# Strassen sums of the activations made beside the second branch and kept in memory

## The chip, the cores and the metric

The kernel runs on one core of a Trainium2 chip. The metric is the device time of one execution in microseconds, the median of several runs. A profiled execution gives a trace, from which a page and the answers to questions are made; its times are microseconds unless marked ns.

Engines are named as in the profile: PE multiplies matrices, DVE (VectorE) and ACT (ScalarE) work on elements, SP only issues transfers here, and ACT issues some as well. SPq and ACTq are those issuing queues.

## The reference

The reference is one layer of an encoder over two sequences, a prompt of 512 and a sample of 256 tokens, each with 16 learned tokens in front, at width 2048:

```python
def mixer_layer(z, norm_g, w_in, ...):
    h = rmsnorm(z, norm_g)
    cols = h @ w_in
    u_a, gate_a, q_b, k_b, v_b, gate_b, glr_b, x_c, gate_c, merge = split_cols(cols)
    y_a = s5_mixer(u_a, ...) * jax.nn.silu(gate_a)
    y_b = gla_mixer(q_b, k_b, v_b, glr_b, ...) * jax.nn.silu(gate_b)
    y_c = rglru_mixer(x_c, ...) * jax.nn.silu(gate_c)
    gates = jax.nn.sigmoid(merge).reshape(bsz, length, N_BRANCH, D_MODEL)
    m = (gates[:, :, 0] * (y_a @ w_out_a) + gates[:, :, 1] * (y_b @ w_out_b)
         + gates[:, :, 2] * (y_c @ w_out_c))
    return z + m @ w_o
```

A final rmsnorm follows, and the learned tokens are dropped. `merge` alone has 3 x 2048 columns, which are 48 of the 84 column blocks of 128 of the input projection.

## The kernel before

Everything is kept transposed: 128 channels on the partitions, tokens along a row. The normalised activations are 16 chunks of 128 channels, each as two tiles `xh[k]` and `xl[k]` of a rounded type (the value is hi + lo), with 784 columns: 16 learned tokens and 768 others. A product with weights takes three matmuls: hi by hi, lo by hi, hi by lo. `split` makes the two parts: ACT copies the value into hi, DVE subtracts hi from the value into lo. The activations are also kept in memory unsplit, as `xnorm` (16 x 128 x 768).

The program runs in stages: input projection and normalisation; branch one (`branch_s5`); branch two (`branch_gla`); branch three (`branch_lru`); the Strassen pairs (`strassen`); the merge of the branches and the output projection (`merge_and_project`).

The 36 column blocks of the branches and the 48 merge blocks are computed in two ways.

- A merge tile (`fill_step`, line 273) is one column block by all 16 chunks: 16 steps of 6 matmuls of 384 columns into two PSUM banks, 96 in all. Its result goes to `gspill` in memory. Such tiles are used to fill PE's time: `tick` puts a step in during branch one at a rate set by `FILLS` (the rates of branches two and three are 0), and `cover` puts in a number of steps outright, such as `LT` = 39 near the end of branch three.
- A Strassen pair is two column blocks at once. Chunks k and k + 8 and the two halves of the 768 columns make a 2 x 2 matrix of blocks, and seven products in place of eight give both results: 4 steps (`sb`) of 7 x 2 x 3 = 42 matmuls, 168 in all, into seven PSUM banks (`products`, line 1149). The eight pairs of gate blocks come first, then `NST` pairs of merge blocks: 8 + 15 = 23. The other 18 merge blocks are merge tiles.

The pairs need four sums of activation blocks for each k from 0 to 7: `sh[0]`, `sh[1]`, `sh[2]` (and `sl`) and a last one, which takes the place of the second half of `xh[k]` and `xl[k]` once the merge tiles no longer need it. `strassen` makes them on DVE, with splits, from `xnorm` loads issued at line 1581, while `cover` lets PE run the remaining merge tiles. Then each step's weights are loaded at line 1615 (`raw`, two buffers), three of them split into hi and lo, and four sums of weights (`t`) split as well; hi and lo have three buffers. Steps are prepared two or three ahead.

A scheduler orders each engine's instructions from the order of the code, and each engine and each issuing queue then runs its own list strictly in order. Transfers of SP carry eight completion counters in turn, so at most eight are under way. A tile whose memory was another tile's waits for the last use of that one.

After the last pair, 16 loads of 192 KB (line 1674) bring back eight branch results into the memory of the sums, they are split, and the merge begins at line 1292.

The functions that the change touches, and what calls them:

Of the kernel before, what the change touches and what calls it, by code (L numbers as in the profile page):

```python
# [6 lines left out]
F32 = mybir.dt.float32  # L7
F32R = mybir.dt.float32r
I32 = mybir.dt.int32
AF = mybir.ActivationFunctionType  # L10
ALU = mybir.AluOpType
# [5 lines left out]
NT = NP_ + NS  # L17
# [3 lines left out]
HN = NT // 2  # L21
# [5 lines left out]
NST = 15  # L27
# [4 lines left out]
XS = 2  # L32
# [63 lines left out]
def build(tc, A, out_p, out_s):  # L96
# [9 lines left out]
    yspill = drm.tile([16, 128, NT], F32, name="yspill")  # L106
    hspill = drm.tile([16, 128, NT], F32, name="hspill")
    zspill = drm.tile([8, 128, NS], F32, name="zspill")
    xnorm = drm.tile([16, 128, NT], F32, name="xnorm")

# [628 lines left out]
def branch_gla(E):  # L739
    tc, A = E["tc"], E["A"]  # L740
    V, S, PE, SP = E["V"], E["S"], E["PE"], E["SP"]
    col, split, proj, evac, tick, psB = (E[k] for k in ("col", "split", "proj", "evac", "tick", "psB"))
# [11 lines left out]
    def tmp():  # L754
        return lp.tile([128, T], F32, name="tmp", bufs=4)

# [25 lines left out]
    for hp in range(2):  # L782
# [139 lines left out]
        for h in range(2):  # L922
# [22 lines left out]
            tick()  # L945
    lp.release()
# [613 lines left out]
def strassen(E):  # L1560
# [11 lines left out]
    sh, sl = [[None] * 8 for i in range(3)], [[None] * 8 for i in range(3)]  # L1572
    for k in range(8):
        for i in range(3):
            sh[i][k] = sp.tile([128, HN], F32R, name=f"sh{i}{k}")
            sl[i][k] = sp.tile([128, HN], F32R, name=f"sl{i}{k}")
    xp = tc.alloc_tile_pool(name="stx", bufs=1, reuse_waits="tile")

    def load(k, o, n, **kw):
        x = xp.tile([128, n], F32, **kw)  # L1580
        (S if k % 8 < XS else SP).dma_start(x[:], xnorm[k, :, o:o + n])
        return x[:]

    def sums(k):
        xa = load(k, 0, NT, name="xa", bufs=2)
        s_, x, u = load(k + 8, HN, HN, name="x", bufs=2), xa[:, :HN], xa[:, HN:]
        V.tensor_tensor(out=s_, in0=s_, in1=u, op=add)
        split(sh[0][k][:], sl[0][k][:], s_)
        V.tensor_tensor(out=s_, in0=s_, in1=x, op=sub)
        split(sh[1][k][:], sl[1][k][:], s_)  # L1590
        V.tensor_tensor(out=u, in0=u, in1=x, op=sub)
        split(sh[2][k][:], sl[2][k][:], u)

    def last_sum(k):

        x = load(k + 8, 0, HN, name="x", bufs=2)
        s_ = xp.tile([128, HN], F32, name="y", bufs=2)[:]
        V.tensor_tensor(out=s_, in0=sh[1][k][:].bitcast(F32), in1=sl[1][k][:].bitcast(F32), op=add)
        V.tensor_tensor(out=s_, in0=x, in1=s_, op=sub)
        split(xh[k][:, t2], xl[k][:, t2], s_)  # L1600

    n = max(1, len(merges))
    for k in range(8):
        sums(k)
        while len(merges) > max(1, n * (7 - k) // 8):
            E["cover"](16)
    E["cover"](16 * len(merges) + 16)

    xp.release()
    tp = tc.alloc_tile_pool(name="stt", bufs=1, reuse_waits="tile")  # L1610
    xp = tc.alloc_tile_pool(name="sty", bufs=2, reuse_waits="tile")
# [14 lines left out]
    def operand(a, k):  # L1626
        if isinstance(a, int):
            return sh[a][k][:], sl[a][k][:]
        tk, ts = k + 8 * (a[1] == "2"), t1 if a[0] == "1" else t2
        return xh[tk][:, ts], xl[tk][:, ts]  # L1630

    ahead = []
    for sb in range(4):
        if sb < 3:
            ahead.append(weights(0, sb))
        last_sum(2 * sb)
        last_sum(2 * sb + 1)
    xp.release()
# [28 lines left out]
    free = [f"s{p}{i}{k}" for k in range(8) for i in range(3) for p in "hl"]  # L1667
    yh, yl = [], []
    for k in range(8):
        h = E["act"].tile([128, NT], F32R, name=f"h{8 + k}")  # L1670
        l = E["act"].tile([128, NT], F32R, name=f"l{8 + k}")
        for o in (0, HN):
            yr = sp.tile([128, HN], F32, name=free.pop(0))
            SP.dma_start(yr[:], E["yspill"][k, :, o:o + HN])
            split(h[:, o:o + HN], l[:, o:o + HN], yr[:])
        yh.append(h)
        yl.append(l)
# [118 lines left out]
```

## Time and profile before

| | us |
|---|---|
| median of three runs | 2037.04 |
| lowest and highest run | 2035.94, 2038.36 |
| the profiled execution: time | 2038.42 |
| the profiled execution: span of the trace | 2036.6 |
| PE busy in the span | 2003.8 (98%) |
| DVE busy | 1504.9 (74%) |
| ACT busy | 808.2 (40%) |

The span lies inside the time: 1.8 us of the profiled execution are outside it. Busy time of PE counts overlapping matmuls once. The stages in this trace: branch one to about 404 us, branch two to about 610, branch three to about 800, the pairs from 842 to 1518, then the rest.

### The profile page before, as it was taken

The numbers are of one execution on the slowest core, as the hardware profiler recorded it, in microseconds if no ns is written. First come the engines' busy times: TensorE is split into PE (matmuls) and PEld (weight loads), VectorE is DVE, ScalarE is ACT, GpSimd is POOL, SyncE is SP. The second block draws the span as 40 slices with busy tenths as digits, with TensorE's granted clock in tenths as the row PEclk, the third lists the DMA queues.
The fourth block names the chain that finished last, engine by engine and source line by source line (L and its number), as shares of the span: only waits on it lengthen the run. The fifth ranks groups of instructions, "written<-read, shape, count | busy, mean of one in ns | idle before, by whom it ended". The sixth has DMA issues, their size and how long they took to land.

```text
span 2036.6 us, 30982 instructions
## 1 busy us (share of the span) xinstructions
PE 2003.8 (98%) x12228; PEld 1972.5 (97%) x12228; DVE 1504.9 (74%) x2784; ACT 808.2 (40%) x1172; POOL 0.2 (0%) x4
## 2 busy tenths in 40 slices
PE   8999999999999999999999999999999999999997
PEld 8999999999989999999999999999999999999997
DVE  8988983656567876977676656665669989887778
ACT  7332111443437675433333222222235435533345
POOL 0000000000000000000000000000000000000000
PEclk9999999999999999999999999999999999999999
DMA  8762234421111323543443222322355335532256
GB/s 292 251 123 94 75 102 120 147 80 49 61 52 45 102 72 122 179 133 102 139 135 112 94 94 100 103 91 100 104 183 215 125 114 180 176 117 94 94 163 218
DMA packets 105378, 252.12 MB, mean 124 GB/s; under 512 B 18960, under 2 KB 39952, under 8 KB 105232
## 3 DMA queue, kind: packets, MB, share of 16 engines
q1 hardware_dynamic: 77072, 200.61, 30.8%
q10 hardware_dynamic: 28160, 49.53, 6.9%
q8 instruction: 96, 1.57, 0.3%
q14 instruction: 50, 0.41, 0.1%
HBM read 200.65 MB, written 49.45 MB: 123 GB/s over the span
## 4 chain that ended last, share of the span: by engine, by line
PE 78%; DVE 13%; ACT 4%; DMA 3%; issue 1%; ACTq 0%; SPq 0%; DVEq 0%
PE pm L1149 24%; PE br L1149 23%; PE pm L199 10%; PE pm L273 5%; PE br L1422 4%; PE pm L1292 2%; PE br L1292 2%; DVE sc L61 2%; DVE W L61 2%; PE pm L332 2%; DVE lo L61 2%; ACT gt L89 1%; DMA c<-gspill 1%; DVE hb L61 1%; PE br L199 1%
## 5 line engine op out<-in xcount | busy, mean ns | idle before, releaser
L89 ACT ACTIVATE hi<-raw 128x768 fp32r<-128x768 f32 (+2 forms) x234 | 216.1, 924 | 482.8 <-PE br L1149 129.0
L61 DVE TENSOR_TENSOR lo<-raw,hi 128x768 fp32r<-128x768 f32 (+2 forms) x234 | 246.3, 1053 | 131.5 <-ACT hi L89 131.1
L61 DVE TENSOR_TENSOR lo<-t,hi 128x1024 fp32r<-128x1024 f32 x140 | 171.5, 1225 | 193.4 <-ACT hi L89 193.2
L89 ACT ACTIVATE hi<-t 128x1024 fp32r<-128x1024 f32 x140 | 148.4, 1060 | 279.6 <-PE pm L1149 138.3
L1149 PE MATMUL pm<-l,hi 128*128 128x384 f32 (+1 forms) x616 | 197.3, 320 | 0.0
L1149 PE MATMUL pm<-h,hi 128*128 128x384 f32 (+1 forms) x616 | 196.6, 319 | 0.2 <-ACT g L89 0.2
L1149 PE MATMUL pm<-h,lo 128*128 128x384 f32 (+1 forms) x616 | 196.6, 319 | 0.0
L1149 PE MATMUL br<-l,hi 128*128 128x384 f32 (+1 forms) x504 | 167.1, 331 | 0.0
L1149 PE MATMUL br<-h,hi 128*128 128x384 f32 (+1 forms) x504 | 165.9, 329 | 0.0
L1149 PE MATMUL br<-h,lo 128*128 128x384 f32 (+1 forms) x504 | 165.8, 329 | 0.0
L199 PE MATMUL pm<-h,hi 128*128 128x392 f32 (+1 forms) x608 | 161.8, 344 | 1.2 <-ACT xp L1022 1.2
L199 PE MATMUL pm<-h,lo 128*128 128x392 f32 (+1 forms) x608 | 159.5, 342 | 1.0 <-DVE lo L61 1.0
L199 PE MATMUL pm<-l,hi 128*128 128x392 f32 (+1 forms) x608 | 159.6, 341 | 0.0
L273 PE MATMUL pm<-h,lo 128*128 128x384 f32 x512 | 131.6, 338 | 2.5 <-DVE lo L61 2.5
L273 PE MATMUL pm<-h,hi 128*128 128x384 f32 x512 | 133.8, 342 | 0.0
L273 PE MATMUL pm<-l,hi 128*128 128x384 f32 x512 | 132.6, 340 | 0.0
L1149 PEld LDWEIGHTS pm<-h,hi 128*128 128x128 f32 x616 | 115.7, 188 | 0.7 <-ACT g L89 0.5
L1149 PEld LDWEIGHTS pm<-h,lo 128*128 128x128 f32 x616 | 116.0, 188 | 0.0
L1149 PEld LDWEIGHTS pm<-l,hi 128*128 128x128 f32 x616 | 115.7, 188 | 0.0
L199 PEld LDWEIGHTS pm<-h,hi 128*128 128x128 f32 x608 | 111.0, 188 | 2.7 <-ACT xp L1022 1.5
L199 PEld LDWEIGHTS pm<-h,lo 128*128 128x128 f32 x608 | 111.2, 188 | 1.5 <-DVE lo L61 1.3
L199 PEld LDWEIGHTS pm<-l,hi 128*128 128x128 f32 x608 | 110.6, 188 | 0.2
(358 smaller groups left out, 4799.6 us busy)
## 6 DMA issues: line engine op xcount, KB each, us to landing
raw<-in_w_st SPq DMA_DIRECT2D x92, 512.0 KB
raw<-in_w_in SPq DMA_DIRECT2D x74, 512.0 KB
gspill<-g ACTq DMA_DIRECT2D x48, 384.0 KB
raw<-in_w_ost SPq DMA_DIRECT2D x32, 512.0 KB
xr<-in_xT SPq DMA_DIRECT2D x31, 392.0 KB
m<-gspill SPq DMA_DIRECT2D x26, 384.0 KB
raw<-in_w_out SPq DMA_DIRECT2D x16, 512.0 KB
raw<-in_w_outc SPq DMA_DIRECT2D x16, 512.0 KB
```

Of the source, the lines that this page charges most:

```text
L61: return f(*a, **k)
L89: ins = self.eng.activation(**k)
L199: PE.matmul(ps[h][:, :nw], w[:, k, :], xx[kt][:, n0 + h * nw:n0 + (h + 1) * nw], start=(kt == 0 and j == 0), stop=(kt == 15 and j == 2))
L273: PE.matmul(ps[h][:, :HN], w[:, k % 8, :], xx[k][:, NM + h * HN:NM + (h + 1) * HN], start=(k == 0 and j == 0), stop=(k == 15 and j == 2))
L332: PE.matmul(ps0[2 * t + h][:, :HT], w[:, k, :], xx[kt][:, h * HT:(h + 1) * HT], start=(kt == 0 and j == 0), stop=(kt == 15 and j == 2))
L1149: PE.matmul(ps[j][:, :nt], w[:, wi, kk, :], x, start=(k == 0 and q == 0), stop=(k == n - 1 and q == 2))
L1292: PE.matmul(ps[h][:, :HN], w[:, 4 * b + k, :], yy[4 * b + k][:, h * HN:(h + 1) * HN], start=(k == 0 and j == 0), stop=(k == 3 and j == 2))
L1422: PE.matmul(po[:, :NS], x[:, n, :], y[k][:, ss], start=(first and j == 0), stop=(last and j == 2))
```

## The change

The four sums of each k are made in branch two, by the new `strassen_sums`, which is called at every third `tick` of that branch: it loads two chunks of `xnorm`, makes the sums in place in two tiles of 768 columns (`pa`, `pb`), splits each (hi into `ph`, lo in place) and stores the four parts in memory (`sspill`). At the pairs, `fetch` loads three split sums of each k into new tiles (`s1h`, `s1l`, and `s2h`, `s2l` with two sums side by side), and `fetch_last` loads the fourth into the second half of `xh[k]` and `xl[k]`. The sums on DVE between branch three and the pairs are gone, with their covers. `NST` is 16: 16 merge tiles in place of 18, and 24 pairs in place of 23. After the pairs, eight loads of 384 KB bring back the branch results into the `s2` tiles.

```diff
-NST = 15
+NST = 16
-XS = 2
...
+    sspill = drm.tile([8, 2, 2, 128, NT], F32, name="sspill")
...
+    def strassen_sums(k):
+        a, b = (lp.tile([128, NT], F32, name=n) for n in ("pa", "pb"))
+        SP.dma_start(a[:], E["xnorm"][k])
+        SP.dma_start(b[:], E["xnorm"][k + 8])
+        t1, t2 = slice(0, HN), slice(HN, NT)
+        TT = lambda o, x, y, op: V.tensor_tensor(out=o, in0=x, in1=y, op=op)
+        TT(b[:, t2], b[:, t2], a[:, t2], ALU.add)
+        TT(a[:, t2], a[:, t2], a[:, t1], ALU.subtract)
+        TT(a[:, t1], b[:, t2], a[:, t1], ALU.subtract)
+        TT(b[:, t1], b[:, t1], a[:, t1], ALU.subtract)
+        for i, x in enumerate((a, b)):
+            h = lp.tile([128, NT], F32R, name="ph")
+            S.activation(out=h[:], in_=x[:], func=AF.Copy)
+            TT(x[:].bitcast(F32R), x[:], h[:].bitcast(F32), ALU.subtract)
+            SP.dma_start(E["sspill"][k, i, 0], h[:].bitcast(F32))
+            SP.dma_start(E["sspill"][k, i, 1], x[:])
+
+    beside = [k for k in range(8)]
+    ticks = [0]
+
+    def tick():
+        E["tick"]()
+        ticks[0] += 1
+        if ticks[0] % 3 == 0 and beside:
+            strassen_sums(beside.pop(0))
...
-    def sums(k):
-        xa = load(k, 0, NT, name="xa", bufs=2)
-        s_, x, u = load(k + 8, HN, HN, name="x", bufs=2), xa[:, :HN], xa[:, HN:]
-        V.tensor_tensor(out=s_, in0=s_, in1=u, op=add)
-        split(sh[0][k][:], sl[0][k][:], s_)
-        V.tensor_tensor(out=s_, in0=s_, in1=x, op=sub)
-        split(sh[1][k][:], sl[1][k][:], s_)
-        V.tensor_tensor(out=u, in0=u, in1=x, op=sub)
-        split(sh[2][k][:], sl[2][k][:], u)
...
+    def fetch(k):
+        s1[k] = [sp.tile([128, HN], F32R, name=f"s1{p}{k}") for p in "hl"]
+        s23[k] = [sp.tile([128, 2, HN], F32R, name=f"s2{p}{k}") for p in "hl"]
+        for p in range(2):
+            SP.dma_start(s1[k][p][:].bitcast(F32), spill[k, 1, p, :, HN:])
+            SP.dma_start(s23[k][p][:].bitcast(F32), spill[k, 0, p].rearrange("q (i n) -> q i n", i=2))
+
+    def fetch_last(k):
+        for p, x in enumerate((xh, xl)):
+            SP.dma_start(x[k][:, t2].bitcast(F32), spill[k, 1, p, :, :HN])
+
     for k in range(8):
-        sums(k)
-        while len(merges) > max(1, n * (7 - k) // 8):
-            E["cover"](16)
+        fetch(k)
     E["cover"](16 * len(merges) + 16)
...
-        last_sum(2 * sb)
-        last_sum(2 * sb + 1)
+        fetch_last(2 * sb)
+        fetch_last(2 * sb + 1)
...
-        for o in (0, HN):
-            yr = sp.tile([128, HN], F32, name=free.pop(0))
-            SP.dma_start(yr[:], E["yspill"][k, :, o:o + HN])
-            split(h[:, o:o + HN], l[:, o:o + HN], yr[:])
+        yr = sp.tile([128, NT], F32, name=f"s2{'hl'[k % 2]}{k // 2}")
+        SP.dma_start(yr[:], E["yspill"][k])
+        split(h[:], l[:], yr[:])
```

SP's list at the hand-over from branch three to the pairs, before: `in_w_in` are merge tile weights, `xnorm` the activations for the sums, `in_w_st` the weights of a pair's step, in the order of the steps.

```order
L135 DMA raw<-in_w_in 128x1024 x8
L1581 DMA xa<-xnorm 128x768
L1581 DMA x<-xnorm 128x384
L1581 DMA xa<-xnorm 128x768
L1581 DMA x<-xnorm 128x384
L1615 DMA raw<-in_w_st 128x1024
L1581 DMA xa<-xnorm 128x768
L1581 DMA x<-xnorm 128x384
L1581 DMA xa<-xnorm 128x768
L1581 DMA x<-xnorm 128x384
L1615 DMA raw<-in_w_st 128x1024
```

The same place of the changed kernel, its beginning: the weights of the first two steps, the last sums of chunks 0 to 4 (`l_104` and `h_103` are `xl[0]` and `xh[0]`, and so on), and the first of the other sums.

```order
L135 DMA raw<-in_w_in 128x1024 x4
L1623 DMA raw<-in_w_st 128x1024 x2
L1614 DMA l_104<-sspill 128x384
L1614 DMA h_103<-sspill 128x384
...
L1614 DMA h_206<-sspill 128x384
L1614 DMA l_207<-sspill 128x384
L1608 DMA s1h_7668<-sspill 128x384
L1609 DMA s2h_7670<-sspill 128x768
L1608 DMA s1l_7669<-sspill 128x384
L1609 DMA s2l_7671<-sspill 128x768
```

And its end, where the loads of the sums of chunk 7, the 29th to 32nd, are followed by the weights of the third step, the last sums of chunks 5 to 7, and the weights of the fourth and later steps.

```order
L1608 DMA s1h_7724<-sspill 128x384
L1609 DMA s2h_7726<-sspill 128x768
L1608 DMA s1l_7725<-sspill 128x384
L1609 DMA s2l_7727<-sspill 128x768
L1623 DMA raw<-in_w_st 128x1024
L1614 DMA h_227<-sspill 128x384
L1614 DMA l_228<-sspill 128x384
L1614 DMA h_248<-sspill 128x384
L1614 DMA l_249<-sspill 128x384
L1614 DMA h_269<-sspill 128x384
L1614 DMA l_270<-sspill 128x384
L1623 DMA raw<-in_w_st 128x1024 x5
```

Weights of steps stood between the loads before; now those of the third step stand behind all 32 loads of the sums.

DVE's list in branch two, in the first of the two loops over six blocks of tokens (`am` takes the masked scores, `qsp`, `qip` and `ek` are operands of the score matmuls), in the changed kernel:

```order
L60 TENSOR_TENSOR qip_4037<-ei,qq 64x2x128
L60 TENSOR_TENSOR pa<-pa,ph 128x768
L60 TENSOR_TENSOR ek<-ek,kk 128x256
L60 COPY_PREDICATED am_4039<-masks,br 128x256 x2
L60 TENSOR_TENSOR pb<-pb,ph 128x768
L60 TENSOR_TENSOR at<-am_4039 128x256
L60 TENSOR_TENSOR qsp_4041<-dm,qq 64x2x128
```

The two subtractions of one set of sums now stand between the operands of the scores; the other operations in this piece were there before.

## Rows read from the trace of the kernel before

**Rows 1.** The page: the span, and each engine's busy time, share and instructions.

```profile
span 2036.6 us, 30982 instructions
PE 2003.8 (98%) x12228; PEld 1972.5 (97%) x12228; DVE 1504.9 (74%) x2784; ACT 808.2 (40%) x1172; POOL 0.2 (0%) x4
```

**Rows 2.** PE's waits from 800 us on: releaser, us in total, times, longest.

```profile
PE pm L1149 <- DVE lo L61: 0.8, 1, 0.8
...
PE pm L1149 <- ACT g L89: 0.2, 1, 0.2
```

**Rows 3.** Busy us (instructions) by engine, clock, DMA share, GB/s, during the pairs.

```profile
1000.00:1100.00 100.00, 100.00 (x575) 100.00 (x574) 71.51 (x111) 33.08 (x42) 0.00 (x0) 1.00 0.38 125
```

**Rows 4.** Groups of PE from 750 to 842 us; then PE's timeline, start and us.

```profile
L273 PE MATMUL pm<-l,hi 128*128 128x384 f32 x160 | 41.3, 338 | 0.0
...
842.08 0.51 PE L273 MATMUL pm<-h,lo 128*128 128x384 f32 x2
842.43 0.34 PE L1149 MATMUL br<-h,hi 128*128 128x384 f32 x1
...
849.05 0.45 PE L1149 MATMUL pm<-h,hi 128*128 128x384 f32 x1 [0.17 <-ACT g L89]
...
854.67 0.45 PE L1149 MATMUL pm<-sh,lo 128*128 128x384 f32 x1 [0.78 <-DVE lo L61]
```

**Rows 5.** Groups of DVE and ACT, 800 to 842 us: count, busy us, mean ns.

```profile
L61 DVE TENSOR_TENSOR x<-x,xa 128x384 f32<-128x384 f32 x16 | 8.6, 554 | 9.1 <-DMA x<-xnorm 9.1
L61 DVE TENSOR_TENSOR lo<-raw,hi 128x768 fp32r<-128x768 f32 x1 | 1.0, 953 | 0.0
...
L89 ACT ACTIVATE hi<-raw 128x768 fp32r<-128x768 f32 x1 | 0.8, 842 | 0.0
```

**Rows 6.** Branch two: two stretches as in rows 3, waits of DVE and PE.

```profile
400.00:600.00 200.00, 197.84 (x1106) 184.59 (x1105) 124.19 (x248) 77.08 (x144) 0.00 (x0) 1.00 0.17 58
560.00:580.00 20.00, 19.58 (x120) 17.18 (x119) 19.24 (x53) 7.16 (x17) 0.00 (x0) 1.00 0.00 1
DVE lo L61 <- ACT hi L89: 30.5, 9, 7.4
PE br L906 <- DVE qsp L61: 0.4, 2, 0.2
```

**Rows 7.** The waits of SP's queue from 430 to 610 us.

```profile
SPq L135 <- DVE lo L61: 161.4, 14, 27.1
```

**Rows 8.** Timeline of DVE at the end of branch three.

```profile
797.22 1.01 DVE L61 TENSOR_TENSOR hb<-hb,hf 128x512 f32<-128x512 f32 x2
```

**Rows 9.** SP's timeline, then the chain that ended last: issue to landing.

```profile
810.13 0.33 SPq L1581 DMA_DIRECT2D xa<-xnorm  x1
...
810.55 3.53 DMA x<-xnorm
```

**Rows 10.** Stretches of 10 us as in rows 3, with the DMA engines busy.

```profile
10.00:20.00 10.00, 9.74 (x53) 9.30 (x53) 9.81 (x11) 9.91 (x13) 0.00 (x0) 1.00 1.03 409
80.00:90.00 10.00, 10.00 (x58) 10.00 (x56) 10.00 (x12) 5.84 (x8) 0.00 (x0) 1.00 1.01 353
810.00:820.00 10.00, 10.00 (x59) 10.00 (x58) 8.79 (x18) 5.19 (x11) 0.00 (x0) 1.00 0.76 245
1500.00:1510.00 10.00, 10.00 (x59) 10.00 (x58) 7.31 (x11) 4.45 (x7) 0.00 (x0) 1.00 0.86 290
1530.00:1540.00 10.00, 10.00 (x59) 10.00 (x58) 9.37 (x18) 7.67 (x12) 0.00 (x0) 1.00 1.02 402
```

**Rows 11.** Timelines of SP and PE where the pairs end.

```profile
1502.92 0.43 SPq L1674 DMA_DIRECT2D sl<-yspill  x1
...
1518.60 0.34 PE L1292 MATMUL br<-h,hi 128*128 128x384 f32 x1
```

More of the change, by code (lines that the diff above doesn't have):

```diff
@@ L741, in branch_gla @@
     V, S, PE, SP = E["V"], E["S"], E["PE"], E["SP"]
-    col, split, proj, evac, tick, psB = (E[k] for k in ("col", "split", "proj", "evac", "tick", "psB"))
+    col, split, proj, evac, psB = (E[k] for k in ("col", "split", "proj", "evac", "psB"))
     ones, ident = E["ones"], E["ident"]
@@ L945, in branch_gla @@
             tick()
+    assert not beside
     lp.release()
@@ L1571, in strassen @@
     sp = tc.alloc_tile_pool(name="st", bufs=1, reuse_waits="tile")
-    sh, sl = [[None] * 8 for i in range(3)], [[None] * 8 for i in range(3)]
-    for k in range(8):
[L1574 to L1582, printed above, removed]
-    def sums(k):
-        xa = load(k, 0, NT, name="xa", bufs=2)
-        s_, x, u = load(k + 8, HN, HN, name="x", bufs=2), xa[:, :HN], xa[:, HN:]
-        V.tensor_tensor(out=s_, in0=s_, in1=u, op=add)
-        split(sh[0][k][:], sl[0][k][:], s_)
-        V.tensor_tensor(out=s_, in0=s_, in1=x, op=sub)
-        split(sh[1][k][:], sl[1][k][:], s_)
-        V.tensor_tensor(out=u, in0=u, in1=x, op=sub)
-        split(sh[2][k][:], sl[2][k][:], u)
[L1594 to L1603, printed above, removed]
-        sums(k)
-        while len(merges) > max(1, n * (7 - k) // 8):
-            E["cover"](16)
+    s1, s23, spill = {}, {}, E["sspill"]
+    def fetch(k):
[7 more added lines that the diff above has]
+            SP.dma_start(x[k][:, t2].bitcast(F32), spill[k, 1, p, :, :HN])
+    for k in range(8):
+        fetch(k)
     E["cover"](16 * len(merges) + 16)
-    xp.release()
     tp = tc.alloc_tile_pool(name="stt", bufs=1, reuse_waits="tile")
-    xp = tc.alloc_tile_pool(name="sty", bufs=2, reuse_waits="tile")
     def weights(i, sb):
@@ L1627, in operand @@
         if isinstance(a, int):
-            return sh[a][k][:], sl[a][k][:]
+            return (s1[k][0][:], s1[k][1][:]) if a == 0 else (s23[k][0][:, a - 1], s23[k][1][:, a - 1])
         tk, ts = k + 8 * (a[1] == "2"), t1 if a[0] == "1" else t2
@@ L1635, in strassen @@
             ahead.append(weights(0, sb))
-        last_sum(2 * sb)
-        last_sum(2 * sb + 1)
-    xp.release()
+        fetch_last(2 * sb)
+        fetch_last(2 * sb + 1)
     xp = tc.alloc_tile_pool(name="stu", bufs=1, reuse_waits="tile")
@@ L1665, in strassen @@
             S.dma_start(E["gspill"][d, :, b, :], g[:])
-    free = [f"s{p}{i}{k}" for k in range(8) for i in range(3) for p in "hl"]
     yh, yl = [], []
```

## Prediction

> **What bounds the kernel now.** I read the page's first part, then the waits of PE over the whole span. PE is busy for 2003.8 of 2036.6 us [rows 1], and in the long middle part it has almost no waits: of the 23 Strassen pairs two waits are listed, 0.8 and 0.2 us [rows 2]. So PE's matmul stream is the bound there. The mean duration of one matmul on the page can't be used as a price, because matmuls overlap; the price is the rate of a stretch with nothing else in it: 575 matmuls of 384 columns in 100 us, 0.174 us each [rows 3]. Next I looked at the place that the change rebuilds, the hand-over from the third branch to the first pair. After the last gate matmuls PE runs 480 matmuls of merge tiles, three groups of 160, which are five tiles [rows 4]. The first pair starts at 842.43 and has the two waits named above, 0.17 and 0.78 us. While PE covers, VectorE makes the sums there, and none of it shows as a wait of PE.
>
> **Matmuls removed and added.** Two merge tiles are 2 x 16 x 6 = 192 matmuls, one pair is 4 x 42 = 168. The built order shows just that: 192 fewer at the merge line, 168 more at the products' line, and nothing else changed in number. 24 x 0.174 = **-4.2 us**. The two tiles that vanish from PE's order are the last two before the first pair. So the first pair now starts 192 x 0.175 = 33.6 us earlier, at 808.8, if all before it stays (a step of two matmuls takes 0.35 us in rows 4).
>
> **Sums at the hand-over removed.** Their DVE and ACT time was hidden under the five cover tiles; taking it away gives back the 0.95 us of waits in the first pair: **-1.0 us**, at best, since those were waits on split results that came behind the last sums. If they stay, 0.
>
> **Sums in the second branch added.** One of the eight sets is four additions of 384 columns at 0.55 us, two subtractions of 768 at 0.95, and two ACT copies of 768 at 0.84 [rows 5]: 4.1 us of DVE, 1.7 us of ACT; all eight 33 and 13 us. Between 400 and 600 us VectorE is busy 124 of 200 us while PE is full [rows 6], and the largest item in its idle time is 30.5 us in nine waits for a weight split (up to 7.4 us each). In the new order most of the sums stand round such a split, so they fall into these holes. Only in the dense part, the six blocks with the masked scores, there is little room: 560 to 580 has DVE at 19.24 of 20. There two subtractions (1.9 us) stand inside each of the two loops, as the piece of VectorE's order shows, with some further additions at their edges. The order also moves PE's score matmuls behind about eight more projection matmuls (1.4 us) there, which covers most of it; before, PE waited 0.4 us in all for these operands. What is late would be the score matmuls, with projections queued behind them in PE's order. Bounds: 0, if the holes take everything; 6 us, if in both loops 1.9 us and one further set's edge (about 1.1 us) appear unhidden. I take **+1 us**, near the low end, since the row with 0.4 us shows how closely that order keeps up.
>
> SP's queue in this branch now carries 48 more transfers (two loads, four stores, eight times), and the stores wait for ACT and DVE ahead of weight loads. SP now waits 161 us in 14 waits there for raw buffers [rows 7], so weights are loaded as soon as a buffer frees, with hi and lo buffers full ahead of PE: some 17 us (two halves of 48 matmuls) lie between a split and its use. A store would have to block for longer than that. I put 0 on it.
>
> **The reload, the term that decides.** Each pair step (42 matmuls, 7.3 us) needs its weights split and the sums of two chunks. The first pair's third step is due at 808.8 + 2 x 7.3 = 823.4. SP's new order is: weights of steps one and two; ten loads of 192 KB into the activation tiles, each held until the last cover tile's matmuls of that chunk are done; all 32 loads of the sums; only then the weights of the third step. Nothing of these 32 is needed by that step alone, but its weights can't overtake them. The last cover tile runs from 792.0 to 808.8, so its first chunk is free at 793.1. The sums' tiles lie over the third branch's memory, whose last addition ends at 798.2 [rows 8]; that holds back little.
> Bytes up to and with these weights: 10 x 0.197 + 8 x (2 x 0.197 + 2 x 0.393) + 0.52 = 11.9 MB. For the fixed part of a load I take a 192 KB load that landed 3.53 us after its issue with 384 KB issued just ahead [rows 9]: 0.59 MB at 350 GB/s is 1.7 us, so 1.8 us remain. For the rate I have stretches of 10 us [rows 10]: 409 and 402 GB/s with the 16 engines full and rows of 3 KB or more, 353 full with stores among the loads, 290 at 0.86 busy with 192 KB loads (337 if full), and 245 at 0.76 on the very loads that the change drops. A third of the sums' bytes move in 192 KB loads: 3.15 / 337 + 6.29 / 402 GB/s is 25 us, 378 GB/s; but about 0.8 MB of stores (a gate tile, a branch result) share the engines, so I take 350, nearest to the full row with stores.
> 793.1 + 1.8 + 11.9 / 0.350 = 829.0 for the landing; then the split, 0.84 on ACT and 0.95 on DVE: 830.8. The wait of the third step is 830.8 - 823.4 = **+7.4 us**. Lower end: the sums start at 797.3, when the fifth chunk is free, and 9.96 MB (the sums and these weights) flow at 409: 797.3 + 1.8 + 24.4 + 1.8 = 825.3, a wait of 2. Upper end at 245 throughout: 845.4, a wait of 22. Steps one and two are safe in the middle case: chunks 0 and 1 (2.4 MB) land by about 808, needed at 812. The fourth step's weights have 1.7 MB behind the third's, 4.8 us, less than a step.
>
> On this the Trainium skill has a figure that would change a chance: "DMA: Bandwidth & Descriptors", section Specifications, gives about 358 GB/s as the limit between HBM and one core. By it the lower end would be a wait of 5.3 us (an estimate from that page: 9.96 MB in 27.8 us, in place of 24.4), and the faster rival below would be out. The rows with 402 and 409 GB/s disagree, so I keep it.
>
> **The end of the pairs.** The results are reloaded as eight loads of 384 KB into the sums' tiles of chunks 0 to 3, so half of them wait one step longer than now. Before, the last was issued at 1502.92 and the projection began at 1518.60 with no wait [rows 11]. One step is 7.3 us; 4 x 0.393 + 0.52 MB take 6 us, so they are in by some 8 us before PE needs them. The last splits wait for PE anyway, not for loads. 0.
>
> **Sum.** -4.2 - 1.0 + 7.4 + 1.0 = +3.2 us. The profiled execution had a span of 2036.6 and a time of 2038.42; with the sum 2039.8 and 2041.6. The median of the runs is 2037.04, 1.4 under the profiled one; on it the forecast is 2040.2, which I round to **2040**. That is within 0.2% (4.1 us, about what a measurement can tell from no change here): no change, leaning slower.
>
> **Rivals.**
> *Reload hidden.* If the stream runs at 402 to 409 GB/s from 797.3 and the second branch takes nothing, the sum is -4.2 - 1.0 + 2 = -3.2, or -5.2 with no wait at all: 2032 to 2034. For it: two stretches at that rate. Against it: they had rows of 3 KB or more and few stores.
> *Slow reload (ends slower).* One mechanism: the loads of the sums run at the 245 GB/s of the xnorm loads. The wait is 22 us, the sum +17.8, 2055; between, at 320, 11.9 MB take 37.2 us and the wait is 10.5: 2043. It decides from a wait of 8.3 us, which is a rate of 341. For it: just these shapes showed 245. Against: there, the engines were busy only 0.76, so the buffers paced them, not the engines.
> *Second branch lags.* The sums in the dense loops delay the scores by 3 to 6 us more than I took: 2043 to 2046. For it: 19.24 of 20 us. Against: 20 us later DVE is half idle, and PE has projections to run.
>
> **How the numbers follow.** Forecast (wait 3 to 10, branch 0 to 3): 0.56, its own range 2035 to 2043, and a quarter of it (0.14) lies above 2041.1. Reload hidden 0.13, about half of it (0.07) under 2033. Slow reload 0.15. Second branch lags 0.16. So faster 0.07, within 0.2% 0.42 + 0.06 = 0.48, slower 0.14 + 0.15 + 0.16 = 0.45. The range leaves out the lowest part of the hidden reload and the upper half of the slow one: 2033.5 to 2048.
>
> **What would show it.** In the changed kernel's trace: the products' line with 6048 matmuls and the merge line with 1344; PE at 192 matmuls less up to the first pair, which starts near 809; one wait of some 7 us of PE at that pair's 85th matmul, ended by the split of weights that SP issued after the sums, and none of size at steps one, two, four; 10 us stretches from 795 to 830 with the DMA engines near full at about 350 GB/s; between 400 and 610 waits of PE on score operands of about 1 us. I am wrong if the third step's weights land before 822 (then faster), or if PE waits in the second branch for more than 4 us, or if the first two steps also wait, which would mean a rate near 245.

## The result and the profile after

The changed kernel takes 2049.81 us (median of six runs, 2048.82 to 2052.1) against 2037.13 for the kernel before (six runs on the same chip): ratio 1.0063, 95% interval 1.005 to 1.0076. It is slower by 12.7 us. The forecast was 2040, no change, with a range up to 2048: wrong. The profiled execution has a time of 2049.04 and a span 10.6 us longer than that of [rows 1].

The page of the changed kernel, span and busy times; PE has 24 matmuls fewer and nearly as much to do:

```profile
span 2047.2 us, 31028 instructions
PE 2001.0 (98%) x12204; PEld 1968.8 (96%) x12204; DVE 1510.6 (74%) x2775; ACT 805.5 (39%) x1149; POOL 0.2 (0%) x4
```

PE's timeline of both executions where a stage begins (start, us): branch two's first gate-up matmul, branch three's first gate matmul, the first pair, the merge. First the kernel before (its first pair and its merge are in [rows 4, 11]), then the changed one.

```profile
420.79 0.82 PE L793 MATMUL br<-glr,wup 128*128 128x392 f32 x2
618.50 0.53 PE L1053 MATMUL br<-xch,gwh 128*128 128x402 f32 x2
```
```profile
421.26 0.82 PE L821 MATMUL br<-glr,wup 128*128 128x392 f32 x2
624.65 0.54 PE L1082 MATMUL br<-xch,gwh 128*128 128x402 f32 x2
813.44 0.34 PE L1178 MATMUL br<-h,hi 128*128 128x384 f32 x1
1528.62 0.52 PE L1321 MATMUL br<-h,hi 128*128 128x384 f32 x2
```

So the 10.6 us are made up like this. Up to branch two: +0.5. Branch two: 203.4 for 197.7, **+5.7**. From there to the first pair: 188.8 for 223.9, which is 33.6 for the two tiles and 1.5 more. From the first pair to the merge: 715.2 for 676.2, **+39.0**, of which one more pair is 29.4 (675.2 / 23), and the two waits of [rows 4] are gone (-1.0); 10.6 are lost there. After that: +0.6.

The 1.5 us are no merit of the change. Granted clock (the third figure from the end) in one stretch of branch three, before and after:

```profile
750.00:770.00 20.00, 18.08 (x94) 17.73 (x93) 12.89 (x15) 10.20 (x16) 0.00 (x0) 0.91 0.21 72
```
```profile
750.00:770.00 20.00, 18.10 (x102) 17.78 (x101) 15.91 (x22) 7.54 (x15) 0.00 (x0) 1.00 0.27 93
```

With PE as busy (18.08 and 18.10 us), TensorE ran a part of that stretch at the lower of its two levels, 1.2 GHz, in the one execution and not in the other. The same shows in the traces of four of the runs below (sums unsplit, set moved, GpSimd's queue, second buffers), with 190.3 us from branch three to the first pair instead of 188.8. It would account for most of the 2 us by which the medians differ more than the spans.

**The reload.** SP's timeline, PE's waits and timeline, and stretches of 10 us as in [rows 10]:

```profile
797.53 0.33 SPq L1614 DMA_DIRECT2D l<-sspill  x1
...
804.60 0.46 SPq L1608 DMA_DIRECT2D s1h<-sspill  x1
...
829.18 0.32 SPq L1609 DMA_DIRECT2D s2l<-sspill  x1
829.76 0.33 SPq L1623 DMA_DIRECT2D raw<-in_w_st  x1
```
```profile
837.46 0.69 PE L1178 MATMUL br<-h,hi 128*128 128x384 f32 x1 [9.20 <-ACT hi L88]
837.94 0.52 PE L1178 MATMUL br<-l,hi 128*128 128x384 f32 x1
838.26 0.52 PE L1178 MATMUL br<-h,hi 128*128 128x384 f32 x1
...
841.05 0.34 PE L1178 MATMUL br<-l,hi 128*128 128x384 f32 x1
841.23 0.34 PE L1178 MATMUL br<-h,lo 128*128 128x384 f32 x1
```
```profile
800.00:810.00 10.00, 10.00 (x59) 10.00 (x58) 5.24 (x9) 1.05 (x1) 0.00 (x0) 1.00 0.97 330
810.00:820.00 10.00, 10.00 (x59) 10.00 (x58) 4.95 (x6) 2.68 (x5) 0.00 (x0) 1.00 1.01 366
820.00:830.00 10.00, 8.26 (x48) 7.94 (x46) 0.00 (x0) 0.00 (x0) 0.00 (x0) 1.00 1.04 399
830.00:840.00 10.00, 2.54 (x7) 2.17 (x8) 2.32 (x4) 1.82 (x2) 0.00 (x0) 0.54 0.96 357
```

The third step's weights are issued behind all 32 loads, and PE waits for their split: one wait, 9.2 us. Behind it the matmuls start 0.32 us apart up to 841.05 and 0.17 to 0.18 from there, and the granted clock is 0.54 from 830 to 840: most of that stretch lies at 1.2 GHz. 10.6 - 9.2 leaves 1.4 us for this.

**Branch two.** VectorE's, SP's and PE's timelines at the second head pair, then a stretch of the changed kernel:

```profile
559.43 0.56 DVE L60 TENSOR_TENSOR pb<-pb,pa 128x384 f32<-128x384 f32 x1 [5.62 <-DMA pb<-xnorm]
559.91 1.84 DVE L60 TENSOR_TENSOR tmp<-tmp,kk 128x784 f32<-128x784 f32 x2
```
```profile
550.24 0.32 SPq L774 DMA_DIRECT2D sspill<-pb  x1
552.19 0.32 SPq L761 DMA_DIRECT2D pa<-xnorm  x1
554.07 0.32 SPq L762 DMA_DIRECT2D pb<-xnorm  x1
```
```profile
561.02 0.99 PE L880 MATMUL br<-ident,tmp 128*128 128x128 f32 x4 [3.52 <-DVE tmp L60]
```
```profile
560.00:580.00 20.00, 18.70 (x99) 15.85 (x100) 17.54 (x47) 5.30 (x12) 0.00 (x0) 0.91 0.06 22
```

The first addition of a set waits 5.62 us for its load, which SP could issue only when the store of the set before had left `pb`. Behind it in VectorE's order stand the key products (`tmp<-tmp,kk`), and PE's transposes wait for these, with projections queued behind. Here too the clock is lower afterwards: 0.91, 99 matmuls in 20 us where [rows 6] has 120.

PE's waits in this branch add up to 5.4 us, against 1.6 before: 3.8 of the 5.7. A clock of 0.91 over 20 us is worth some 1.8 more (an estimate, 0.09 x 20). The two together are what the branch lost.

### The profile page after: what moved, and what is told of

Read it like the earlier page. It is cut to its first block, busy times and chain, and to the rows that moved or that the text cites. A ratio compares the mean times of both kernels' runs of the same rounds, so it can differ in the third digit from the quotient of the medians.

```text
span 2047.2 us, 31028 instructions
## 1 busy us (share of the span) xinstructions
PE 2001.0 (98%) x12204; PEld 1968.8 (96%) x12204; DVE 1510.6 (74%) x2775; ACT 805.5 (39%) x1149; POOL 0.2 (0%) x4
## 4 chain that ended last, share of the span: by engine, by line
PE 74%; DVE 14%; DMA 6%; ACT 4%; issue 1%; SPq 0%; ACTq 0%; DVEq 0%
PE br L1178 24%; PE pm L1178 22%; PE pm L273 7%; PE pm L199 6%; PE pm L1451 3%; DVE sc L60 2%; DVE W L60 2%; DVE lo L60 2%; PE br L1321 2%; PE pm L332 2%; PE pm L1321 1%; PE br L1451 1%; DVE m L60 1%; ACT gt L88 1%; DMA sspill<-pb 1%
## 5 line engine op out<-in xcount | busy, mean ns | idle before, releaser
L60 DVE TENSOR_TENSOR lo<-t,hi 128x1024 fp32r<-128x1024 f32 x144 | 176.3, 1224 | 205.6 <-ACT hi L88 205.5
L1178 PE MATMUL br<-h,hi 128*128 128x384 f32 (+1 forms) x576 | 187.3, 325 | 9.4 <-ACT hi L88 9.2
L1178 PE MATMUL br<-l,hi 128*128 128x384 f32 (+1 forms) x576 | 188.2, 327 | 0.4 <-DVE l L60 0.4
L1178 PE MATMUL br<-h,lo 128*128 128x384 f32 (+1 forms) x576 | 187.3, 325 | 0.0
L1178 PEld LDWEIGHTS br<-h,hi 128*128 128x128 f32 x576 | 108.4, 188 | 10.0 <-ACT hi L88 9.5
L60 DVE TENSOR_TENSOR t<-raw 128x512 f32<-128x512 f32 x144 | 99.0, 688 | 23.6 <-DMA raw<-in_w_st 17.6
L273 PE MATMUL pm<-l,hi 128*128 128x384 f32 x448 | 116.1, 340 | 0.0
L199 PEld LDWEIGHTS pm<-h,hi 128*128 128x128 f32 x608 | 111.3, 188 | 2.6 <-ACT xp L1051 1.5
L199 PEld LDWEIGHTS pm<-h,lo 128*128 128x128 f32 x608 | 111.2, 188 | 1.6 <-DVE lo L60 1.3
L199 PEld LDWEIGHTS pm<-l,hi 128*128 128x128 f32 x608 | 111.0, 188 | 0.2
L1178 PEld LDWEIGHTS br<-h,lo 128*128 128x128 f32 x576 | 108.9, 189 | 0.4 <-DVE lo L60 0.4
```

What stands on the lines that cost most here:

```text
L60: return f(*a, **k)
L199: PE.matmul(ps[h][:, :nw], w[:, k, :], xx[kt][:, n0 + h * nw:n0 + (h + 1) * nw], start=(kt == 0 and j == 0), stop=(kt == 15 and j == 2))
L273: PE.matmul(ps[h][:, :HN], w[:, k % 8, :], xx[k][:, NM + h * HN:NM + (h + 1) * HN], start=(k == 0 and j == 0), stop=(k == 15 and j == 2))
L1178: PE.matmul(ps[j][:, :nt], w[:, wi, kk, :], x, start=(k == 0 and q == 0), stop=(k == n - 1 and q == 2))
```

## The experiments

Two lengths of the profiled executions, in us, are compared: branch two (first gate-up matmul to the first gate matmul of branch three) and the pairs (first pair to merge). 24 pairs at the speed of the 23 before would take 704.6. The order of branch two is the same in the changed kernel and four runs; it takes 201.6 to 206.9 there. Read as above, these five executions differ mostly by TensorE's clock behind the wait at the transposes (the estimate is the share of clock missing, times the length of the stretch):

| same order of branch two | PE's waits over before | clock, estimate | branch two over before |
|---|---|---|---|
| weights first | 3.6 | 0 | 3.9 |
| changed | 3.8 | 1.8 | 5.7 |
| fourth too | 3.1 | 3.4 | 6.6 |
| idle filled | 4.5 | 3.4 | 8.1 |
| reload early | 4.8 | 5.0 | 9.2 |

The stretch of the first and of the last of them:

```profile
560.00:580.00 20.00, 17.39 (x100) 14.94 (x101) 18.29 (x48) 5.30 (x12) 0.00 (x0) 1.00 0.08 31
560.00:580.00 20.00, 18.45 (x83) 15.39 (x83) 15.22 (x41) 4.88 (x11) 0.00 (x0) 0.76 0.06 22
```

So a difference under some 3 us between two single lengths of this branch tells nothing unless PE's waits and the clock are read beside it. Ratios are to the kernel before on the same chip, 2037.1 to 2038.5 us.

| | time (runs) | ratio, 95% interval | branch two | pairs |
|---|---|---|---|---|
| before | 2037.13 (6) | | 197.7 | 676.2 (23) |
| changed | 2049.81 (6) | 1.005 to 1.0076 | 203.4 | 715.2 |
| weights first | 2049.8 (4) | 1.0042 to 1.0073 | 201.6 | 713.8 |
| fourth too | 2042.84 (10) | 1.0016 to 1.0034 | 204.3 | 709.1 |
| idle filled | 2049.86 (1) | | 205.8 | 713.8 |
| reload early | 2045.94 (5) | 1.0024 to 1.0049 | 206.9 | 710.0 |
| loads a set ahead | 2052.82 (4) | 1.0058 to 1.0089 | 204.6 | 716.4 |
| that and weights first | 2053.95 (5) | 1.0067 to 1.0094 | 205.6 | 713.3 |
| no loads | 2047.62 (1) | | 201.1 | 717.1 |
| sums unsplit | 2043.7 (7) | 1.0021 to 1.0043 | 203.7 | 709.2 |
| no sums | 2043.12 (1) | | 197.7 | 716.6 |
| sums on GpSimd | 2065.03 (1) | | 217.9 | 716.7 |
| that and reload early | 2058.37 (4) | 1.0079 to 1.011 | 216.4 | 710.0 |
| that, one pair less | 2054.05 (5) | 1.0064 to 1.0089 | 217.1 | 674.7 (23) |
| set moved | 2055.22 (1) | | 205.2 | 716.3 |
| set moved, no gap | 2040.69 (11) | 1.0005 to 1.0022 | 203.4 | 705.8 |
| GpSimd's queue | 2063.82 (4) | 1.0114 to 1.0145 | 216.1 | 716.2 |
| that, set moved, no gap | 2053.76 (4) | 1.0066 to 1.0093 | 216.8 | 706.6 |
| work only, no gap | 2037.99 (1) | | 200.0 | 705.8 |
| second buffers, no gap | 2036.52 (11) | 0.9988 to 1.0006 | 198.8 | 705.8 |

### The reload: place in the queue, bytes, clock

**Weights first.**

```diff
-    for k in range(8):
-        fetch(k)
...
+        fetch(2 * sb)
+        fetch(2 * sb + 1)
         fetch_last(2 * sb)
```

> The loads of the sums are issued step by step behind each step's weights, so the third step's weights stand in SP's queue before the loads of chunks 4 to 7 instead of behind all 32. Theory (place in the queue): the wait of 9.2 us and the slow matmuls behind it (1.7 us) go; PE's waits inside the first pair are at most 1 us in all; the merge begins 10 to 11 us before 1528.62, near 1518; time near 2039 by the runs of the changed kernel (2049.8). Rival (rate): the bytes set it whatever their order, and the wait only moves to the sums of chunks 4 to 7 or to the fourth step: 4 to 9 us of waits stay in the first pair, time 2044 to 2049.

PE's waits at the pairs' line over the run, and two stretches:

```profile
PE br L1178 <- ACT hi L88: 5.6, 1, 5.6
```
```profile
830.00:840.00 10.00, 5.88 (x31) 4.99 (x29) 0.00 (x0) 0.00 (x0) 0.00 (x0) 1.00 1.05 393
840.00:850.00 10.00, 7.66 (x29) 7.32 (x30) 6.42 (x11) 3.00 (x4) 0.00 (x0) 0.66 0.22 77
```

The theory fell as stated. The wait of the third step went, and one of 5.6 us came at the fourth, whose weights now stood last, with slow matmuls behind it. I had not counted what the whole first pair needs by about 835: the prediction's 11.9 MB, six more loads of 0.197 and the fourth step's weights, 13.6 MB.

**The fourth step too**: the weights of three steps first, those of the fourth ahead of chunks 6 and 7.

> As the run with the weights first, and the fourth step's weights stand ahead of the loads of chunks 6 and 7 too. Theory now (bytes and place): all that the first pair needs, some 13.6 MB, has to come between 797.5 and about 835; at 365 to 380 GB/s that takes 36 to 37 us, so what was lost at the fourth step (a wait of 5.6 us and slow matmuls behind it) shrinks to a wait of 0 to 2.5 us; the merge begins at 1518 to 1521, against 1526.98 and 1528.62. Rival (rate alone, order without effect): 5 us of waits or more stay in the first pair, the merge begins at 1525 or later.

The merge began at 1522.49, between the two, and five waits of at most 1.07 us were left. SP's timeline shows a gap of 4 us, in which SP stood on the third step's `raw`, whose buffer was not free, with the DMA engines at 286 GB/s from 810 to 820:

```profile
806.11 0.32 SPq L1609 DMA_DIRECT2D s2h<-sspill  x1
810.29 0.33 SPq L1621 DMA_DIRECT2D raw<-in_w_st  x1
```

**Reload early**: SP's order fixed by hand, the sums of chunks 0 and 1 before the loads that wait for the last merge tile.

> SP's order at the pairs is fixed: weights of two steps, then the sums of chunks 0 and 1, which go into memory that the third branch leaves early, before the loads that wait for the last merge tile; then step by step, with the third and fourth step's weights between. Theory (bytes and place): the stream starts by 793 instead of 797.5 and has no gap, all is in by about 831, no wait over 1 us is left in the first pair, and from the first pair to the merge it takes 704.5 to 706.5 us (715.2 now, 709.1 with the fourth step's weights early). Rival (the memory of the third branch is free only at 798 to 802): 2 to 5 us of waits stay, 707 to 710 us. The second branch is as it was: time 2038 to 2041.

The stream began at 793.5, but stood still twice (796.9 to 803.8, 804.8 to 808.8): 710.0 us, the rival. By the waits of SP's queue these stops ended, after 6.5 and 3.7 us, with the stores of the third branch's last results (`hspill<-hb`), which ACT's queue issued only at 799.34 and 805.56. A third stop, of 5.6 us up to 823.7, ended with the store of a gate tile. What ties these loads to these stores was not tested.

**The place without a gap** (with a set of sums moved, below):

```diff
-    for k in range(8):
-        fetch(k)
...
-    for sb in range(4):
-        if sb < 3:
-            ahead.append(weights(0, sb))
...
+    ahead = [weights(0, sb) for sb in range(2)]
+    for k in range(8):
+        fetch(k)
+        fetch_last(k)
+        if k in (2, 5):
+            ahead.append(weights(0, 2 + k // 5))
...
```

> The moved set, and at the pairs the third step's weights behind the sums of three chunks and the fourth's behind six. The earlier order had a gap of 4 us in the stream, in which SP stood on the third step's weights. Theory: without the gap and without the place at the end of the queue the first pair has waits of at most 1 us in all, 704.5 to 706.5 us from the first pair to the merge (715.2 in the changed kernel); time 2036 to 2041. Rival (the bytes need longer than PE gives them whatever the order): 3 us of waits and more, 708 us or more.

705.8 us, as expected, and no wait of a step for its weights at the first pair is left over 1 us. The same bytes, in the order in which they are needed, cost 1.2 us instead of 10.6:

```profile
800.00:810.00 10.00, 10.00 (x59) 10.00 (x58) 5.30 (x9) 0.88 (x1) 0.00 (x0) 1.00 0.98 332
810.00:820.00 10.00, 10.00 (x59) 10.00 (x59) 4.95 (x6) 2.85 (x5) 0.00 (x0) 1.00 0.99 366
820.00:830.00 10.00, 10.00 (x59) 9.90 (x58) 3.64 (x5) 1.90 (x2) 0.00 (x0) 1.00 1.05 399
830.00:840.00 10.00, 9.80 (x55) 9.23 (x54) 4.10 (x6) 2.39 (x3) 0.00 (x0) 1.00 1.05 390
```

**Idle filled** (50 matmuls into a bank that the second pair uses later):

```diff
...
+            if i == 0 and sb == 2:
+                for r in range(50):
+                    PE.matmul(spare[:, :HN], xh[0][:, NM:NM + 128], xh[0][:, t1], start=True, stop=True)
```

> 50 matmuls that nobody reads stand in PE's order between the second and the third step of the first pair, in the place of the wait of 9.2 us. Theory (TensorE's clock falls in the wait): the granted clock stays at 1.0 from 830 to 850, the matmuls behind run 0.17 us apart at once, and the merge begins 1.5 us earlier, near 1527.1. Rival (the slow matmuls come from the loads that still run, or from the splits): they run 0.32 us apart until about 841 all the same, and the merge begins near 1528.6.

```profile
839.73 0.45 PE L1178 MATMUL br<-h,hi 128*128 128x384 f32 x1 [0.57 <-ACT hi L88]
```
```profile
830.00:840.00 10.00, 9.43 (x54) 9.11 (x53) 1.12 (x3) 0.84 (x1) 0.00 (x0) 1.00 1.05 390
840.00:850.00 10.00, 9.96 (x57) 9.64 (x57) 7.54 (x11) 4.30 (x5) 0.00 (x0) 1.00 0.50 171
```

The clock stays at 1.00 although the loads run as before, and the pairs take 1.4 us less. (The merge began at 1529.47, not 1527.1, because the first pair began 2.2 us later, at 815.66.) So the idle time of PE cost 1.4 us more than its wait here.

### Branch two: place, work, transfers

**Loads a set ahead**, two buffers each (`pb` in the memory of `g`), and the same with the weights first.

> The two chunks of each set of sums are loaded one set ahead into two buffers each; sums, splits and stores are the same. Theory (VectorE stands on a load, with the products that PE's transposes need behind it): the 17.5 us that VectorE waited for these loads go to under 4, the 3.9 us wait of PE at the transposes goes to under 1, the first pair starts near 809 instead of 813.3, time near 2045.5. Rival (the sums' own work in VectorE's full stretch): PE still waits 3 to 5 us in this branch and the first pair starts at 812 to 814, time near 2049.

> Both edits together. If the two waits are independent and nothing else cost time, the gains add: first pair near 809, merge near 1513.5, time 2034 to 2035.5, that is 2 to 3 us under the kernel before. If the reload is bound by the rate, an earlier first pair only makes its wait longer: 2040 to 2045.

Missed. VectorE waited less for loads (5.5 us instead of 17.5), but the scheduler moved the sums forward, and at one place they stood ahead of what frees the banks for the gate-up matmuls:

```profile
516.15 0.56 DVE L60 TENSOR_TENSOR g<-g,pa 128x384 f32<-128x384 f32 x1 [2.07 <-DMA g<-xnorm]
...
519.68 0.96 DVE L60 TENSOR_TENSOR g<-g,ph 128x768 fp32r<-128x768 f32 x1 [1.20 <-ACT ph L88]
520.55 1.02 DVE L60 TENSOR_SCALAR tmp<-br 128x384 f32<-128x384 f32 x2
```
```profile
521.16 2.98 PE L829 MATMUL br<-glr,wup 128*128 128x392 f32 x4 [3.08 <-DVE tmp L60]
```

**No loads, no sums.**

> Leaves out seven of the eight pairs of loads of activations in the second branch (the sums are made over and over on the first two tiles); VectorE's and ScalarE's work and the stores stay. Theory (load): no wait of VectorE for these loads, PE's wait at the transposes under 1 us, the first pair near 809. Rival (work): as in the changed kernel, 812 to 814. The reload and its wait of about 9 us are not touched.

> Leaves out the sums and splits in the second branch; the loads and the stores stay (the loaded chunks themselves are stored). Theory (VectorE's and ScalarE's order): with nothing of the sums in these orders PE waits there for none of them, and the first pair starts at 808.5 to 809.3. Rival (the 48 transfers, by holding up the weights): the first pair starts at 810.5 or later. The wait at the third step stays, 9 to 10 us.

Without loads 201.1 us, with a wait of PE of 2.0 us for ScalarE in place of those for VectorE and the clock at 0.91 behind it; without sums 197.7, to the tenth as before the change. So the 48 transfers by themselves cost nothing: the 5.7 us come only with the sums.

**Sums unsplit** (half the bytes at the pairs, VectorE's work halved):

> The sums are kept unsplit in memory and split when they come back, and they come back step by step: the reload carries 8.4 MB with the weights instead of 13.6, the second branch has only the four additions of each set (18 us of VectorE instead of 33, no ScalarE, half the stores). Theory: all loads are in by 825, no wait over 1 us in the first pair; the second branch loses less than now, the first pair starts at 809 to 812; the merge begins at 1514 to 1517, time 2035 to 2038. Rival: the splits at the pairs stand in front of the weights' splits on VectorE and ScalarE, and 3 to 8 us of waits come back at the steps: time 2040 to 2046.

203.7 us: half the work and the same length. PE's waits are 2.9 us over those before instead of 3.8, and the clock took the rest (0.83 from 460 to 480). At the pairs 709.2, the rival: splits of sums stood ahead of what PE needed (1.5 us for one of them).

**A set moved** (27th step of the branch instead of the 18th).

```diff
-        if ticks[0] % 3 == 0 and beside:
+        if ticks[0] in (3, 6, 9, 12, 15, 21, 24, 27):
```

> One set of sums is made at the 27th step of the second branch instead of the 18th, so that in VectorE's order no set stands between the key products of the second head pair and what they wait for (only earlier). The same work, loads and stores. Theory (place: what stands ahead of the instructions that PE waits for): PE's wait at the key transposes goes under 1 us and the second branch (first gate-up matmul to the first gate matmul of the third) takes 199 to 202 us; five executions of the changed order took 201.6 to 206.9. Rival (the amount of work, wherever it stands): 203 to 207 us, the wait only turns up elsewhere.

Missed: PE's wait at the key transposes fell to 1.3 us, one of 3.9 came at the transposes of the values. The place alone is not it.

**GpSimd: sums, or transfers only.**

```diff
+        G = tc.nc.gpsimd
-        TT = lambda o, x, y, op: V.tensor_tensor(out=o, in0=x, in1=y, op=op)
+        TT = lambda o, x, y, op: G.tensor_tensor(out=o, in0=x, in1=y, op=op)
...
-            S.activation(out=h[:], in_=x[:], func=AF.Copy)
+            G.tensor_copy(out=h[:], in_=x[:])
```

> The sums and their splits of the second branch run on GpSimd, which had nothing to do; loads, stores and everything else as in the changed kernel. Theory (what costs time there is that these instructions stand in VectorE's and ScalarE's order ahead of those that PE waits for): from the first gate-up matmul of the second branch to the first gate matmul of the third it takes 197.5 to 198.5 us as in the kernel before (203.4 now), and the first pair starts at 807 to 809. Rival (GpSimd works on the same memory as VectorE and slows it, or its sums are so late that stores hold up the weights): 201 us or more. The reload's wait stays or grows: 9 to 14 us.

> The loads and stores of the sums in the second branch are issued by GpSimd's queue, which has nothing else to do, instead of SP's; the sums stay on VectorE and ScalarE. Theory (loads stand in SP's order behind stores and weights that wait): the loads are issued as soon as their buffers are free, VectorE waits for them under 8 us instead of 17.5, PE's wait at the key transposes goes under 1.5, and the branch takes 199 to 202 us. Rival (single buffers, filled only when the stores have landed, set the pace): VectorE waits as long as now or longer and the branch takes 203 us or more.

Both far off, 216 to 218 us. Waits of SP's queue and of ACT in branch two with the sums on GpSimd, and VectorE's splits there from 430 to 600:

```profile
SPq L774 <- POOL ph L772: 77.6, 15, 11.3
```
```profile
ACT hi L88 <- DMA raw<-in_w_in: 26.2, 3, 14.4
```
```profile
L60 DVE TENSOR_TENSOR lo<-raw,hi 128x1024 fp32r<-128x1024 f32 x13 | 17.7, 1360 | 25.7 <-ACT hi L88 22.4 <-PE br L853 3.2
```

Stores that wait for the slower engine (an addition takes 1171 ns there, 553 on VectorE) now hold up the weights in SP's queue, the case that I had put at 0, and VectorE's splits take 1360 ns instead of 1218. The Trainium skill ("GPSIMD Engine Reference", section 1. Specifications) says that GpSimd shares its SBUF interfaces with VectorE, with contention for VectorE instructions that have two inputs there; the trace agrees, since these splits have two. With the transfers alone on that queue, VectorE waited 22.5 us for loads instead of 17.5: a load still follows a store there, and longer. PE's waits in the branch are 13.6 us there and 14.9 with the sums on GpSimd, against 5.4, and the clock is as low as 0.74 and 0.83 over 20 us behind them. How much of this each cause makes was not tested.

The combinations show the same parts:

> Both: sums on GpSimd and the reload early. If both theories hold, what is left of the change is its 24 matmuls and the 0.95 us: the first pair at 807 to 809, the merge at 1512 to 1515, time 2031 to 2034. If the earlier first pair outruns the reload, 2 to 4 us more: 2034 to 2038.

> As the run with both, but 15 merge pairs and 18 merge tiles as before the change (24 matmuls more). If the term for the pair is right, 4.2 us slower than the run with both, 2035 to 2038; if the sum's first term is not earned, the same time.

> GpSimd's queue, the moved set and the reload without gap together. If place and queue are what costs in the second branch: 199 us there, 705 to 706 from the first pair to the merge, time 2033 to 2037, under the kernel before. If not: 2038 to 2043.

The one with a pair less was 4.3 us faster, not slower. In the traces 2.4 us of this lie ahead of branch two, where the two kernels are the same, and 1.8 between branch three and the merge: with 33.6 us more of merge tiles ahead of it the first pair had no wait, 674.7 us; the other lost 5.4 against 704.6, more than the 4.2 of the pair. The pair's gain shows only if the reload is covered.

**The work alone, and second buffers.** Both with the reload without gap.

> The reload without gap; in the second branch all the sums and splits are made (33 us of VectorE, 13 of ScalarE), but over and over on the first two loaded chunks, and stored once: 14 loads and 28 stores are left out. Theory now (not the work but transfers that stand ahead of it in the orders: VectorE waits for loads, ScalarE's copy for the store of the last hi part): the second branch takes 197.5 to 199 us, as without the sums (197.7). Rival (the work itself): 200.5 us or more, as with the seven pairs of loads left out (201.1).

```diff
-        a, b = (lp.tile([128, NT], F32, name=n) for n in ("pa", "pb"))
+        a, b = lp.tile([128, NT], F32, name="pa"), E["gp"].tile([128, NT], F32, name="g")
...
-            h = lp.tile([128, NT], F32R, name="ph")
+            h = lp.tile([128, NT], F32R, name="ph", bufs=2)
```

> The reload without gap; in the second branch one of the two loaded chunks has two buffers and the hi part has two, in the memory that there is. If transfers are what the branch waits for, part of it goes: 199.5 to 202.5 us there (203.4 now), 705.8 from the first pair to the merge, time 2036 to 2039, about the kernel before. If the order only shifts the waits, as with the loads a set ahead: 203 to 206 us, time 2040 to 2043.

The work alone takes 200.0 us, between the two expectations: PE's waits are 2.2 us over those before, and the clock stays at 1.00. With all transfers the five executions above had waits of 3.1 to 4.8 us over, and in four of them the clock fell behind the wait. So both theories have a part: about 2 us go with the work, and the transfers add 1 to 3 us of waits and what the clock then takes, in one execution each. The second buffers bring it to 198.8 with all work and transfers (waits of 1.0 us over, the clock at 1.00), so that no more than 1.1 us was paid for the sums there. The times agree: this kernel differs from the one with the set moved and no gap only in branch two, and eleven runs of each give ratios of 0.9997 and 1.0014. What VectorE still waited for loads, and the wait of PE that came with the sums:

```profile
DVE g L60 <- DMA pa<-xnorm: 5.9, 2, 3.9
```
```profile
PE br L850 <- ACT tmp L88: 1.0, 1, 1.0
```

This kernel computes all that the changed one does and takes 2036.52 us, 13 less, and the same as the kernel before (0.9997): of the 5.2 us to be gained, branch two and the reload still take a good 2, and an interval from -2.4 to +1.2 us does not tell the rest from nothing.

## Why the prediction was wrong

The span grew by 10.6 us, the sum had 3.2. Of the 7.4 between them branch two has 4.7, the reload 1.8, the clock behind the reload 1.4, the start and the end 1.1, less 1.5 for the clock in branch three before.

- **Matmuls, -4.2, and the two waits, -1.0**: right. 24 matmuls fewer, the first pair 33.6 us earlier but for what came ahead, neither wait there any more.
- **The reload, +7.4**: place and mechanism right, one wait, ended by the split of those weights; size 9.2. The first load was issued at 797.5, not 793.1, but the third step was due as much later (828.3, not 823.4), because the first pair itself came late; this cost nothing. The step that was off is the stream: 11.9 MB took until 836.6 (the split's start), with 1.8 fixed 37.2 us instead of 34.1, or 320 GB/s instead of 350. The split then held PE for 0.9 us, not 1.8, since the first matmul waits for ACT's copy alone. The DMA engines were not slower than assumed:

```profile
797.50:836.60 39.10, 30.76 (x177) 30.44 (x175) 12.72 (x19) 4.95 (x9) 0.00 (x0) 0.93 1.00 364
```

  At 364 GB/s they moved 14.2 MB in these 39.1 us, 2.3 more than the prediction counted up to these weights. Two stores of 384 KB and six loads of 192 KB, issued behind the weights but before these had landed, make 2.0 of it. The Trainium skill's 358 GB/s ("DMA: Bandwidth & Descriptors", Specifications) is again passed, with 399 in one stretch.
- **No term for TensorE's clock**: 1.4 us at the reload (shown by the filled wait), and some 1.8 of the 5.7 in branch two, where it stood at 0.91. Waits were priced as if PE took up at full speed.
- **Branch two, +1.0 (0 to 6)**: the step that failed. I priced VectorE's time and laid it into holes. It came to 5.7, and PE's waits there to 5.4 us, over the 4 that I had named as a sign of being wrong. What costs is that these instructions wait, for a load behind a store of the same buffer and for ScalarE's copy behind the store of the hi part, with the ones that PE needs behind them in the order, and that the clock is lower after PE's wait. I looked for it in the score loops; it came at the transposes. With second buffers the branch lost 1.1, near my figure; the work without the transfers lost 2.3. The rival of a lagging branch had the size, 4 to 7 us, by luck: it laid it to the scores in the dense loops.
- **SP's stores, 0**: right for the changed kernel, where ACT did not wait for weights; wrong as soon as stores came later (sums on GpSimd).
- **The end of the pairs, 0**: +0.6.
- **Range**: the cases were held apart. The reload in its upper half and a lagging branch came together, and no chance was given to both at once.

## What to carry to other kernels

Work that moves under another engine's cover is not priced by its busy time alone: look at what each moved instruction waits for, and at what stands behind it in every order it enters; one buffer for load, work and store makes those waits. When data is brought back for a consumer that starts at once, count the bytes up to each of its steps, with what shares the engines meanwhile, and issue in that order, weights included. Add to a wait of TensorE what its clock takes afterwards, and before two single profiles are compared, look whether the clock fell in one of them.

## What was not expected of the hardware

The slow stretch behind a wait did not grow with the wait. At the pairs matmuls were slow for 3.6 us (837.46 to 841.05) after a wait of 9.2 in the changed kernel, for 6.4 us (839.07 to 845.51) after 9.18 in the run with loads a set ahead, and for 5.4 us (842.34 to 847.77) after 5.56 with the weights first. In branch two the clock stayed at 1.00 after a wait of 3.13 us with the weights first, and fell after one of 2.02 us in the run without loads (0.91 from 540 to 560). In branch three of the kernel before it fell after a wait of 1.92 us (0.91 from 750 to 770, worth 1.5 us); the changed kernel has a wait of 1.9 us there too and kept 1.00. So equal waits at the same place can cost differently from one execution to the next.
